# A two-layer encoder trunk: the pooled layer's group map folded into its input weights, and weights kept split between two attentions

## The chip, the cores and the metric

The kernel runs on one core of a Trainium2 chip. The core has a matrix engine (PE), three engines that work on 128 partitions (DVE, ACT and POOL), and a sequencer (SP) that issues nearly all DMAs of this kernel in one queue. The metric is the device time of one execution in microseconds; the kernel before has a median of 2261.05 us over three runs (2259.12 to 2262.42).

## The reference

Two requests (x_prompt and x_sample, 1024 tokens of 1024 channels each) go through the same two layers. Each layer computes modulation rows from c, `mod = silu(c) @ ada_w[l] + ada_b[l]`, splits them into shift, scale and gate, normalises x, applies scale and shift, mixes, normalises again and adds the gated result to x.

Layer 0 mixes by attention: one input projection of 3328 columns feeds eight heads of dilated sliding windows (the A heads) and eight heads of dense attention with two key heads (the B heads); a SiLU gate and an output projection follow. Layer 1 mixes by pooling:

```
u, gate = jnp.split(h @ w_in, 2, axis=-1)
...
pooled = win_sum / cnt - u32.reshape(b, s, POOL_GROUPS, POOL_GROUP_DIM)
mixed = jnp.einsum('bsgc,gcd->bsgd', pooled.astype(h.dtype), w_grp)
mixed = mixed * scale.reshape(POOL_GROUPS, POOL_GROUP_DIM)
y = mixed.reshape(b, s, POOL_WIDTH) * jax.nn.silu(gate)
return y @ w_out
```

There are four groups of 256 channels, with windows of 2, 4, 8 and 16 tokens. Pooling is linear along the tokens and `w_grp` is linear along the channels of a group, so the two may change places.

## The kernel before

Every large product is done on operands split in two: a value is rounded to fp32r (the high half), the rest is the low half, and three matmuls (high by high, high by low, low by high) are added up in PSUM. A weight block is 256 columns by 1024 rows; `load_block` (through `block_gen`, L354) brings it in pieces of 128 x 256 by DMA into a buffer `ws`, of which there are three, and `split` (L346) rounds each piece on DVE (L351) and subtracts on POOL (L352; on DVE for some). Two buffers `w` are used in turn.

The order of work is: the first attention (request "prompt", s = 0), its output projection (`outproj0`), the second attention (s = 1) with its output projection, then the pooled layer (`layer1`) for s = 1 and for s = 0. A scheduler of the framework may reorder instructions that don't depend on one another; `issue_after` and `keep_in_program_order` bind some of them.

**Attention (`layer0`, L641).** Thirteen projection units (one for keys and values, four "P" units for the B heads, eight "A" units), each with one weight block, are cut in 17 steps. The 64 slots of the B heads and the 32 of the A heads drive them: `adv` (L718) takes a unit one step further between the pieces of a slot, so that the block of a coming head is projected while the present head's scores, exponentials, turns and products run. P1 to P3 and A0 are stepped in the B heads' slots, a quarter of them each; A1 to A7 in the A heads'. At step 13 (`marks[-1]`) of one unit, the next one's weights are loaded. In the second attention the key-value unit and P0 run ahead of the slots; P0's weights are loaded unsplit into `raw`, early.

**Modulation rows (`ada_rest`, L214).** During P1 to P3 of the first attention, 16 blocks of 256 columns of `ada_w` are loaded and split by the same helper and multiplied (L225) with the two requests' silu(c), which stands as 34 columns of weights: four blocks for the gate of layer 0 and twelve for layer 1. A small tail per block (L152 to L158, tile `mr`) adds the bias and writes the row to DRAM. In between, `x_ahead` normalises and turns the second request's x.

**The pooled layer (`layer1`, L1202).** For each group: the projection of u (`lin`, L1213 to L1215), pooling in `pool_ct` (window sums on POOL, centring on DVE at L1264, then the split of the pooled mean, L1265 and L1266), the projection of the gate, the output product of the group before (`outp`, L1310 to L1312), and `mixed`: 24 matmuls of the pooled mean with the group's map (L1282 to L1284), the product of scale, map and gate (L1286), and its split (L1289, L1290). PSUM has four tiles "S" for all of them.

Of the kernel before, what the change touches and what calls it, by code (L numbers as in the profile page):

```python
# [13 lines left out]
P = 128  # L14
# [46 lines left out]
class Trunk:  # L61
    def __init__(self, ctx, tc, t):
# [10 lines left out]
        self.raw = None  # L73
# [18 lines left out]
        self.xn_d = self.dram.tile([KT, P, S], F32, name="xn_d")  # L92
        self.v_d = [self.dram.tile([4, 288, P], F32, name=f"v_d{i}") for i in range(3)]
# [36 lines left out]
    def ada_prep(self, pool, b):  # L130
        nc, t = self.nc, self.t
        self.apool = b
# [10 lines left out]
        nc.vector.tensor_tensor(self.cz[:, :, 32:34], csil, self.cz[:, :, 0:2].bitcast(F32), ALU.subtract)  # L143

# [69 lines left out]
    def ada_rest(self, ap):  # L214
        nc = self.nc
        todo = [(l, c, i) for l, c in ((0, 2), (1, 0), (1, 1), (1, 2)) for i in range(4)]
        cur = []

        def step(load):
# [8 lines left out]
            if load and todo:  # L228
                l, c, i = todo.pop(0)
                w = self.load_block(ap, self.ada_src(l, c, i), step=False)  # L230
                row, bias, f = (self.apool.tile([2, 256], F32, name=self.n(x), tag=x, bufs=1)
# [3 lines left out]
                cur.append((w, ps, gen))  # L235

# [117 lines left out]
    def block_gen(self, wp, sp, src, fast=False, step=True, out=None, z=1, bufs=3, tags=("ws",), act=False, raw=None):  # L354
# [6 lines left out]
        for q in range(KT // z):  # L361
            ks = slice(z * q, z * q + z)
            if raw:
                ws = raw[z * q // 4][:, z * q % 4 : z * q % 4 + z]
            else:
                ws = sp.tile([P, z, 256], F32, name=self.n("ws"), tag=tags[q % len(tags)], bufs=bufs)
                nc.sync.dma_start(ws, src[:, ks, :])
            self.split(w[:, 0, ks], w[:, 1, ks], ws, fast and q % 2 == 0, act)
            yield

    def load_block(self, wp, src, fast=False, step=True, z=1, bufs=3, raw=None):
        out = []
        for _ in self.block_gen(wp, wp, src, fast, step, out, z, bufs, raw=raw):
            pass
        return out[0]

# [76 lines left out]
    def unit_A(self, ap, subs, hT, j, out):  # L453
        nc = self.nc
        w = self.load_block(ap, self.t["win"][j])
# [32 lines left out]
        for pr in range(4):  # L488
            ps = self.ptile("J").rearrange("p (a c) -> p a c", a=2)
            yield from self.proj_tile(ps[:, 0, :], hT, w, 2 * pr)  # L490
            if pr == 2:
                trans(0)
            yield
# [49 lines left out]
    def unit_KV(self, ap, subs, hT, out):  # L543
# [21 lines left out]
        for pr in range(4):  # L565
# [4 lines left out]
            todo = []  # L570
            yield
# [23 lines left out]
    def unit_P(self, ap, subs, hT, i, out):  # L595
        nc = self.nc
        raw, self.raw = self.raw, None
        with self.tc.issue_after(self.kvd[0].ins) if raw else ExitStack():
            w = self.load_block(ap, self.t["win"][9 + i], i == 0, raw=raw, z=2 if raw else 1)
# [14 lines left out]
        for pr in range(4):  # L614
            ps = self.ptile("J").rearrange("p (a c) -> p a c", a=2)
            yield from self.proj_tile(ps[:, 0, :], hT, w, 2 * pr)
            if pr == 2:
                trans(0)
            yield
# [21 lines left out]
    def layer0(self, s, hT, ap, side, after_proj, open2, run_h, first=None):  # L641
# [15 lines left out]
        units = [(self.unit_KV(ap, subs, hT, out), 0)]  # L657
        for i in range(4):
            units.append((self.unit_P(ap, subs, hT, i, out), due[("B", 2 * i)]))
        for j in range(8):  # L660
            units.append((self.unit_A(ap, subs, hT, j, out), due[("A", j)]))
# [10 lines left out]
        if s == 1:  # L672
# [3 lines left out]
            self.raw = [ap.tile([P, 4, 256], F32, name=self.n("raw"), tag="P", bufs=3) for _ in range(2)]  # L676
            for f in range(2):
                nc.sync.dma_start(self.raw[f], self.t["win"][9][:, 4 * f : 4 * f + 4, :])
# [28 lines left out]
        with self.tc.issue_after(self.kvd[2].ins):  # L707
            next(gens[2])
# [9 lines left out]
        def adv(ui):  # L718
# [7 lines left out]
            if rest and ui in (2, 3, 4):  # L726
                if k in marks:
                    rest(k != marks[-1])
                else:
# [3 lines left out]
            if k == marks[-1] and ui + 1 < len(gens) and ui + 1 not in started:  # L733
# [338 lines left out]
    def outproj0(self, s, wo, op, hN, pre):  # L1072
# [72 lines left out]
        src = t["pwin"][0] if s else t["win"][8]  # L1145
        for i in range(NT):
            if i == 4:
                self.wi = 1
                self.kvw = self.base.tile([P, 2, KT, 256], F32R, name=self.n("w"), tag="w", bufs=1)
                for q in range(4):  # L1150
# [43 lines left out]
            if i in (5, 6):  # L1194
# [7 lines left out]
    def layer1(self, s, hT, lp, hp, run_h, open_l2):  # L1202
# [3 lines left out]
        wu0 = kvw or self.l1_block(wp, t["pwin"][0])  # L1206
# [32 lines left out]
        def pool_ct(g, ps, p):  # L1239
# [452 lines left out]
```

## Time and profile before

| what | value |
|---|---|
| median of 3 runs | 2261.05 us |
| profiled execution, its own time | 2259.73 us |
| its span | 2257.9 us |
| granted TensorE clock, mean | 0.98 of full speed |
| PE, DVE, ACT, POOL busy | 94%, 70%, 47%, 43% |
| DMA traffic | 193.26 MB, mean 86 GB/s |

The page has the busy time of each engine over the span. A table by stretch shows the same for parts of it; the attention's quarters and the pooled layer's two passes are stretches in what follows. A group of instructions is given with its line, its count, the busy time of all and the mean of one. A timeline lists instructions with their start and duration in us; a bracket behind a row gives the idle time of the engine before it and what ended that.

### The profile page before, as it was taken

The page shows a single profiled execution, that of the slowest core. Times are in us where ns is not written, and L with a number is a line of the kernel's source. Part 1 is how long each engine was busy: PE and PEld are TensorE (multiplying, and loading weights), DVE is VectorE, ACT ScalarE, POOL GpSimd, SP SyncE. Part 2 cuts the span into 40 slices and gives each one's busy share as a digit, 9 for nine tenths or more (in the row PEclk, how much of TensorE's full clock was granted, in tenths as well). Part 3 has the DMA queues.
Part 4 walks back from the last instruction along what each step waited for, and adds up shares of the span by engine and source line. Part 5 has one row for each costly group of instructions (what it writes and reads, how often), then busy time and mean ns, then how long its engine had stood idle before and what let it go on. Part 6 is the DMA issues. An engine that isn't in the chain of part 4 may idle for free.

```text
span 2257.9 us, 38531 instructions
## 1 busy us (share of the span) xinstructions
PE 2114.2 (94%) x13777; PEld 1883.1 (83%) x13777; DVE 1570.6 (70%) x3465; ACT 1065.9 (47%) x2435; POOL 973.5 (43%) x1421
## 2 busy tenths in 40 slices
PE   6998898999999799999999999998999999899998
PEld 3987788989999678998888999996787888788887
DVE  8788888767776855777777777777655455865446
ACT  6445555576666632356666666665322113211112
POOL 3676666104343512653221235334234246573452
PEclk9999999999999799999999999998999999999999
DMA  6134343102121444200011112125433234231113
GB/s 262 45 93 119 94 126 113 52 18 70 54 68 33 126 156 163 67 26 25 11 34 39 44 55 73 52 55 153 144 118 96 73 89 140 108 130 56 47 53 144
DMA packets 156640, 193.26 MB, mean 86 GB/s; under 512 B 16184, under 2 KB 117920, under 8 KB 156448
## 3 DMA queue, kind: packets, MB, share of 16 engines
q1 hardware_dynamic: 156144, 190.01, 26.5%
q8 instruction: 109, 1.79, 0.3%
q10 hardware_dynamic: 304, 0.79, 0.1%
q14 instruction: 83, 0.68, 0.1%
HBM read 148.56 MB, written 42.18 MB: 84 GB/s over the span
## 4 chain that ended last, share of the span: by engine, by line
PE 57%; DVE 20%; POOL 6%; issue 6%; ACT 5%; DMA 5%; SPq 0%; POOLq 0%; DVEq 0%; ACTq 0%
PE J L420 5%; PE J L421 5%; PE J L422 5%; PE S L1213 4%; PE S L1215 4%; PE S L1214 4%; DVE E L771 3%; POOL w L352 3%; PE H L753 3%; DVE w L351 3%; PE S L1022 3%; PE S L1023 3%; DVE mx L754 2%; PE S L1024 2%; PE T L791 2%
## 5 line engine op out<-in xcount | busy, mean ns | idle before, releaser
L352 POOL TENSOR_TENSOR w<-ws,w 128x256 fp32r<-128x256 f32 (+1 forms) x402 | 373.2, 942 | 305.1 <-DVE w L351 232.3
L420 PE MATMUL J<-w,hT 128*128 128x256 f32 x1664 | 481.0, 289 | 3.0 <-ACT xj L433 2.0
L421 PE MATMUL J<-w,hT 128*128 128x256 f32 x1664 | 477.1, 287 | 3.4 <-POOL w L352 2.6
L422 PE MATMUL J<-w,hT 128*128 128x256 f32 x1664 | 475.8, 286 | 4.3 <-DVE hT L1460 3.4
L422 PEld LDWEIGHTS J<-w,hT 128*128 128x128 f32 x1664 | 317.1, 191 | 7.6 <-DVE hT L1460 4.1
L421 PEld LDWEIGHTS J<-w,hT 128*128 128x128 f32 x1664 | 317.7, 191 | 6.5 <-POOL w L352 3.5
L420 PEld LDWEIGHTS J<-w,hT 128*128 128x128 f32 x1664 | 317.4, 191 | 6.5 <-ACT xj L433 3.3
L771 DVE TENSOR_TENSOR E<-T,E 128x512 fp32r<-128x512 f32 x384 | 261.5, 682 | 86.3 <-ACT E L770 84.1
L770 ACT ACTIVATE E<-T 128x512 fp32r<-128x512 f32 x384 | 226.7, 598 | 197.9 <-PE T L791 70.2
L351 DVE CAST w<-ws 128x256 fp32r<-128x256 f32 (+1 forms) x404 | 181.3, 473 | 142.9 <-PE S L1215 74.4
L760 ACT ACTIVATE P<-H,mx 128x512 f32<-128x512 f32 x256 | 173.8, 686 | 100.0 <-DVE mx L755 86.4
L1213 PE MATMUL S<-hT,w 128*128 128x512 f32 x512 | 201.2, 393 | 3.2 <-DVE sg L1271 2.9
L1214 PE MATMUL S<-hT,w 128*128 128x512 f32 x512 | 200.6, 392 | 0.0
L1215 PE MATMUL S<-hT,w 128*128 128x512 f32 x512 | 200.5, 392 | 0.0
L754 DVE TENSOR_REDUCE mx<-H 128x1 f32<-128x512 f32 x256 | 173.5, 681 | 33.5 <-PE H L753 31.6
L791 PE MATMUL T<-identr,P 128*128 128x128 f32 x1024 | 162.4, 274 | 8.1 <-DVE E L771 4.1
L804 PE MATMUL O<-E,v 128*128 128x256 f32 x512 | 143.1, 301 | 13.9 <-DVE E L771 13.2
L870 ACT ACTIVATE P<-H,nm 128x256 f32<-128x256 f32 x256 | 117.9, 474 | 79.5 <-DVE nm L864 79.1
L803 PE MATMUL O<-E,v 128*128 128x256 f32 x512 | 146.9, 296 | 7.6 <-ACT E L770 4.6
L791 PEld LDWEIGHTS T<-identr,P 128*128 128x128 f32 x1024 | 122.2, 141 | 24.4 <-DVE E L771 2.9
L506 POOL TENSOR_TENSOR hl<-xj,hl 128x256 fp32r<-128x256 f32 x64 | 48.4, 758 | 204.7 <-DVE hl L505 148.6
L753 PE MATMUL H<-kh,qT 128*128 128x512 f32 x256 | 112.6, 440 | 8.2 <-ACT P L760 8.1
(278 smaller groups left out, 5133.0 us busy)
## 6 DMA issues: line engine op xcount, KB each, us to landing
ws<-win SPq DMA_DIRECT2D x184, 128.0 KB
ws<-ada_w SPq DMA_DIRECT2D x128, 128.0 KB
ws<-pwin SPq DMA_DIRECT2D x60, 256.0 KB
vb<-v_d SPq DMA_DIRECT2D x64, 144.0 KB
xt<-xp SPq DMA_DIRECT2D x16, 512.0 KB
ada<-ada_w SPq DMA_DIRECT2D x16, 512.0 KB
v_d<-v SPq DMA_DIRECT2D x64, 128.0 KB
wos<-wout SPq DMA_DIRECT2D x32, 256.0 KB
```

The costliest lines, as they stand in the source:

```text
L351: nc.vector.tensor_copy(hi, src)
L352: (nc.vector if dve_lo else nc.gpsimd).tensor_tensor(lo, src, hi.bitcast(F32), ALU.subtract)
L420: nc.tensor.matmul(ps, hi, w[:, 0, k, :], start=(k == 0), stop=False)
L421: nc.tensor.matmul(ps, hi, w[:, 1, k, :], start=False, stop=False)
L422: nc.tensor.matmul(ps, lo, w[:, 0, k, :], start=False, stop=(k == KT - 1))
L754: nc.vector.tensor_reduce(mx[:, c : c + 1], ps[c], axis=AX, op=ALU.max, negate=True)
L770: nc.scalar.activation(ov[0], Tv, AF.Copy)
L771: nc.vector.tensor_tensor(ov[1], Tv, ov[0].bitcast(F32), ALU.subtract)
L791: nc.tensor.transpose(T[:, (2 * e + i) * P : (2 * e + i + 1) * P], Pt[(h, 2 * g + i)][:, (2 * kp + e) * P : (2 * kp + e + 1) * P], self.ident)
L1213: nc.tensor.matmul(ps[:, cs], w[:, 0, k, ws], hT[:, k, 0, cs], start=(k == 0), stop=False)
L1214: nc.tensor.matmul(ps[:, cs], w[:, 0, k, ws], hT[:, k, 1, cs], start=False, stop=False)
L1215: nc.tensor.matmul(ps[:, cs], w[:, 1, k, ws], hT[:, k, 0, cs], start=False, stop=(k == KT - 1))
```

## The change

The change has four parts.

First, `fold` multiplies the map of a group into the u columns of the pooled layer's input weights: for each of four groups and two halves of the rows, 24 matmuls of 256 columns, evacuated by ACT and written to DRAM as `wp_d`. The pooled layer loads `wp_d` in place of the weights; `pool_ct` leaves the pooled (and already mapped) mean in the tile `u`, unsplit, and `gated` multiplies it with scale and gate directly. The 24 matmuls of `mixed`, the split of the pooled mean and the load and split of the map go.

Second, the twelve blocks of modulation rows for layer 1 move from the first to the second attention, as 24 jobs of 128 columns. `aux` gives out these 24 jobs and the eight of the fold, three per unit from P1 to A7: at each call the job that was loaded before is multiplied, and the next is loaded and split into the one buffer `wx`.

Third, the first attention writes each of its 13 split weight blocks to DRAM (`keep_w`, in the second of a unit's four tile pairs), and the second attention reads them back in four DMAs (`w_back`) in place of loading and splitting them. The read of the next unit's block is issued at step 3 of a unit in place of step 13. The key-value block is read back during the output projection of the first attention; P0's early load into `raw` goes.

Fourth, small tiles move (tags `xt` in place of `pT`, three buffers `y1` in place of two).

```diff
-        rest = self.ada_rest(ap) if s == 0 else None
+        if s:
+            self.cz = ap.tile([P, KT, 34], F32R, name=self.n("cz"))
+            nc.sync.dma_start(self.cz.bitcast(F32), self.cz_d)
+        rest = self.ada_rest(ap, ((0, 2),)) if s == 0 else None
+        aux = self.aux(ap) if s else None
...
+            if aux and k in ((3, 8, 13) if ui < 5 else (2, 7, 12)):
+                aux()
-            if k == marks[-1] and ui + 1 < len(gens) and ui + 1 not in started:
+            if k == (3 if s else marks[-1]) and ui + 1 < len(gens) and ui + 1 not in started:
...
+    def aux(self, ap):
+        jobs = [("ada", l, c, i) for l, c in ((1, 0), (1, 1), (1, 2)) for i in range(8)]
+        jobs += [("fold", g, h) for g in range(4) for h in range(2)]
...
+            w = ap.tile([P, 2, KT, P], F32R, name=self.n("wx"), tag="wx", bufs=1)
...
+            for q in range(4):
+                ks = slice(2 * q, 2 * q + 2)
+                ws = ap.tile([P, 2, P], F32, name=self.n("ws"), tag="ws", bufs=3)
+                nc.sync.dma_start(ws, src[:, ks, :])
+                self.split(w[:, 0, ks], w[:, 1, ks], ws)
...
+                for k in range(KT):
+                    for e in range(2):
+                        nc.tensor.matmul(ps[0][0:34], self.cz[:, k, :], w[:, e, k, :], start=(k + e == 0),
+                                         stop=(k + e == KT))
...
+                        for c in range(2):
+                            q = 2 * c + kp
+                            nc.tensor.matmul(o, w[:, 0, q, at], wg[:, 0, c], start=(c == 0), stop=False)
+                            nc.tensor.matmul(o, w[:, 0, q, at], wg[:, 1, c], start=False, stop=False)
+                            nc.tensor.matmul(o, w[:, 1, q, at], wg[:, 0, c], start=False, stop=(c == 1))
...
+    def w_back(self, w, b, pin=lambda x: x):
+        for e in range(2):
+            for f in range(2):
+                sl = slice(KT // 2 * f, KT // 2 * (f + 1))
+                pin(self.nc.sync.dma_start(w[:, e, sl].bitcast(F32), self.w_d[b, :, e, sl]))
...
+    def keep_w(self, s, w, b):
+        if s == 0:
+            self.nc.sync.dma_start(self.w_d[b], w.bitcast(F32))
...
-            nc.vector.scalar_tensor_tensor(wv, wv, 1.0 / WINS[g], u[:, H : H + S], op0=ALU.mult, op1=ALU.subtract)
-            nc.scalar.activation(p[:, 0], wv, AF.Copy)
-            nc.vector.tensor_tensor(p[:, 1], wv, p[:, 0].bitcast(F32), ALU.subtract)
+            p = u[:, H : H + S]
+            nc.vector.scalar_tensor_tensor(p, wv, 1.0 / WINS[g], p, op0=ALU.mult, op1=ALU.subtract)
+            return p
...
-                for c in range(2):
-                    cs = slice(512 * c, 512 * c + 512)
-                    for k in range(2):
-                        nc.tensor.matmul(ps[:, cs], wg[:, 0, k, ws], pT[k][:, 0, cs], start=(k == 0), stop=False)
-                        nc.tensor.matmul(ps[:, cs], wg[:, 0, k, ws], pT[k][:, 1, cs], start=False, stop=False)
-                        nc.tensor.matmul(ps[:, cs], wg[:, 1, k, ws], pT[k][:, 0, cs], start=False, stop=(k == 1))
-                nc.vector.scalar_tensor_tensor(yf, ps, self.sccol[:, 2 * g + ct : 2 * g + ct + 1], sgs[ct],
+                nc.vector.scalar_tensor_tensor(yf, pm[ct], self.sccol[:, 2 * g + ct : 2 * g + ct + 1], sgs[ct],
```

## Rows read from the trace of the kernel before

**Rows 1.** The page, busy us, share of the span, instructions.
```profile
PE 2114.2 (94%) x13777; PEld 1883.1 (83%) x13777; DVE 1570.6 (70%) x3465; ACT 1065.9 (47%) x2435; POOL 973.5 (43%) x1421
```
**Rows 2.** Line 753 by stretch: PE, PEld busy (count), PEclk, DMA share, GB/s.
```profile
106.30:199.60 93.30, 21.07 (x65) 9.97 (x66) 1.00 0.35 102
```
**Rows 3.** Stretches: length, PE, PEld, DVE, ACT, POOL busy (count); PEclk, DMA, GB/s.
```profile
106.00:200.00 94.00, 84.63 (x611) 73.10 (x610) 80.94 (x189) 49.21 (x115) 67.74 (x97) 1.00 0.35 103
200.00:301.00 101.00, 88.06 (x657) 78.06 (x655) 86.40 (x196) 55.66 (x127) 64.37 (x95) 1.00 0.34 101
301.00:405.00 104.00, 96.49 (x728) 88.73 (x725) 85.06 (x199) 54.94 (x126) 64.99 (x96) 0.98 0.37 111
405.00:481.00 76.00, 70.48 (x511) 62.90 (x510) 58.65 (x139) 50.91 (x119) 10.26 (x15) 1.00 0.15 42
481.00:780.00 299.00, 279.96 (x2297) 274.36 (x2296) 219.72 (x736) 196.88 (x526) 124.00 (x259) 0.96 0.22 64
947.00:1028.00 81.00, 80.72 (x633) 76.86 (x632) 61.40 (x134) 44.76 (x105) 42.73 (x67) 1.00 0.10 31
1028.00:1105.00 77.00, 73.40 (x552) 67.41 (x551) 61.29 (x131) 49.04 (x114) 26.18 (x44) 1.00 0.08 22
1105.00:1180.00 75.00, 72.33 (x545) 66.53 (x544) 59.56 (x135) 48.34 (x113) 18.45 (x28) 1.00 0.11 30
1180.00:1250.00 70.00, 64.35 (x452) 56.03 (x451) 56.41 (x131) 49.66 (x116) 9.98 (x14) 1.00 0.11 31
1250.00:1542.00 292.00, 275.81 (x2285) 270.83 (x2284) 216.07 (x731) 195.65 (x524) 123.20 (x258) 0.96 0.22 64
1655.00:1962.00 307.00, 295.97 (x1316) 242.31 (x1315) 170.19 (x175) 65.67 (x82) 138.84 (x125) 0.98 0.31 99
1962.00:2258.00 296.00, 287.90 (x1263) 236.45 (x1261) 163.81 (x154) 46.18 (x56) 145.81 (x113) 1.00 0.26 92
```
**Rows 4.** Line 225 by stretch, columns as in rows 2.
```profile
106.30:199.60 93.30, 18.04 (x96) 10.30 (x96) 1.00 0.35 102
...
301.00:405.00 104.00, 9.75 (x64) 7.00 (x64) 0.98 0.37 111
```
**Rows 5.** Timeline of PE, four short windows: start, duration, instruction.
```profile
1785.89 0.39 PE L1282 MATMUL S<-pT,wg 128*128 128x512 f32 x1
...
1789.16 0.39 PE L1284 MATMUL S<-pT,wg 128*128 128x512 f32 x1
...
123.88 2.06 PE L225 MATMUL T<-w,cz 128*34 128x256 f32 x16
...
748.01 0.46 PE L441 MATMUL T<-identr,hl 128*128 128x128 f32 x4
748.30 0.62 PE L881 MATMUL T<-identr,P 128*128 128x128 f32 x4
```
**Rows 6.** Groups of instructions, shapes apart; the last by tile mr (min/median/max).
```profile
L1282 PE MATMUL S<-pT,wg 128*128 128x512 f32 x64 | 25.4, 396 | 0.0
...
L351 DVE CAST w<-ws 128x256 fp32r<-128x256 f32 x312 | 115.8, 391 | 45.0 <-DMA ws<-win 24.5 <-DMA ws<-ada_w 16.1 <-PE J L422 2.5
...
L352 POOL TENSOR_TENSOR w<-ws,w 128x256 fp32r<-128x256 f32 x308 | 237.0, 782 | 132.5 <-DVE w L351 112.0 <-DVE mx L755 11.2 <-DVE R L815 4.1
...
L153 DVE TENSOR_TENSOR mr<-T,mr x16: 402/404/413, 129.9 to 369.5; 2x256 f32<-2x256 f32 x16
```
**Rows 7.** Timelines of DVE and PE, end of the first pass of the pooled layer.
```profile
1939.20 1.27 DVE L1286 SCALAR_TENSOR_TENSOR yf<-S,sccol,sg 128x1024 f32<-128x1024 f32 x1
...
1941.67 0.79 PE L1310 MATMUL S<-w,y 128*128 128x512 f32 x1 [6.07 <-ACT y L1289]
```
**Rows 8.** Timeline of PE, first group of the first pass.
```profile
1713.72 0.77 PE L1213 MATMUL S<-hT,w 128*128 128x512 f32 x1 [2.94 <-DVE sg L1271]
```
**Rows 9.** Timeline of POOL, ahead of the second attention.
```profile
891.22 3.59 POOL L352 TENSOR_TENSOR w<-y,w 128x512 fp32r<-128x512 f32 x2 [9.39 <-DVE w L351]
```

More of the change, by code (lines that the diff above doesn't have):

```diff
@@ L212, in mod_rows, with ada_rest @@
         nc.sync.dma_start(self.mod_d[0, 1, 0:2].rearrange("c (k p) -> (c k) p", p=P), rows)
-    def ada_rest(self, ap):
+    def ada_rest(self, ap, todo):
         nc = self.nc
-        todo = [(l, c, i) for l, c in ((0, 2), (1, 0), (1, 1), (1, 2)) for i in range(4)]
+        todo = [(l, c, i) for l, c in todo for i in range(4)]
         cur = []
@@ L230, in step @@
                 w = self.load_block(ap, self.ada_src(l, c, i), step=False)
-                row, bias, f = (self.apool.tile([2, 256], F32, name=self.n(x), tag=x, bufs=1)
+                row, bias, f = (ap.tile([2, 256], F32, name=self.n(x), tag=x, bufs=1)
                                 for x in ("mr", "mb", "mf"))
@@ L451, in dup, with unit_A @@
         return f
-    def unit_A(self, ap, subs, hT, j, out):
+    def unit_A(self, s, ap, subs, hT, j, out):
         nc = self.nc
-        w = self.load_block(ap, self.t["win"][j])
+        w = self.win_block(s, ap, j)
         yield
@@ L541, in b_norm, with unit_KV @@
         return x
-    def unit_KV(self, ap, subs, hT, out):
+    def unit_KV(self, s, ap, subs, hT, out):
         nc = self.nc
@@ L570, in unit_KV @@
             todo = []
+            if pr == 1:
+                self.keep_w(s, w, 8)
             yield
@@ L593, in unit_KV, with unit_P @@
         yield
-    def unit_P(self, ap, subs, hT, i, out):
+    def unit_P(self, s, ap, subs, hT, i, out):
         nc = self.nc
-        raw, self.raw = self.raw, None
-        with self.tc.issue_after(self.kvd[0].ins) if raw else ExitStack():
-            w = self.load_block(ap, self.t["win"][9 + i], i == 0, raw=raw, z=2 if raw else 1)
+        w = self.win_block(s, ap, 9 + i, i == 0)
         yield
@@ L656, in layer0 @@
                 due[h] = n
-        units = [(self.unit_KV(ap, subs, hT, out), 0)]
+        units = [(self.unit_KV(s, ap, subs, hT, out), 0)]
         for i in range(4):
-            units.append((self.unit_P(ap, subs, hT, i, out), due[("B", 2 * i)]))
+            units.append((self.unit_P(s, ap, subs, hT, i, out), due[("B", 2 * i)]))
         for j in range(8):
-            units.append((self.unit_A(ap, subs, hT, j, out), due[("A", j)]))
+            units.append((self.unit_A(s, ap, subs, hT, j, out), due[("A", j)]))
         NSTEP = NT * (KT // CK) + 1
@@ L728, in adv @@
                     rest(k != marks[-1])
-                else:
+                elif ahead:
                     next(ahead, None)
@@ L1149, in outproj0 @@
                 self.kvw = self.base.tile([P, 2, KT, 256], F32R, name=self.n("w"), tag="w", bufs=1)
-                for q in range(4):
+                if s == 0:
+                    self.w_back(self.kvw, 8, pin)
+                for q in range(4 * s):
                     ws.append(tile([P, 2, 256], F32, "y0", 4))
@@ L1193, in outproj0 @@
             self.last = added
-            if i in (5, 6):
+            if s and i in (5, 6):
                 for q in (2 * i - 10, 2 * i - 9):
```

121 lines of the change are left out of this document (83 added, 38 removed).

## The prediction

> **What bounds the kernel now.** I began with the page's busy shares: PE is at 94% and DVE, the next engine, at 70% [rows 1], so the question is in which stretches PE itself is the limit. The busy table by stretch answers that. I cut it where the slots of the attention begin: 16 slots of four score matmuls each give one stretch, which the counts of L753 confirm (64 to 65 in each of eight stretches; [rows 2] has the first). The reader is to compare two attentions that do the same work [rows 3]. The second needs 81, 77, 75 and 70 us for its four quarters of B heads and 292 us for its A heads. The first needs 94, 101, 104 and 76, and 299: the A heads agree, the B heads are 72 us longer. What the first has beside them is the modulation rows (16 blocks of 256 columns: L225 has 96 matmuls in each of the first two quarters and 64 in the third [rows 4]) and the normalising of x ahead. In these three quarters DVE is busy 82 to 86% and PE 87 to 93%; in the second attention's four PE has 92 to 100%, and in its A heads it does 2285 matmuls in 292 us. The pooled layer (1655 to 2258) is PE nearly without a gap.
>
> Busy time overstates a matmul here, since the next starts before one ends. So I read prices as start-to-start distances. L1282 to L1284: from 1785.89 to 1789.16 are 14 steps, 0.234 us each [rows 5]. L225, 256 columns: 16 in 2.06 us, less one of 0.28, over 15: 0.119 us. Turning 128 columns in fp32r: 4 in 0.46 us, of 0.24 each: 0.073 us; in fp32 (4 in 0.62 us, of 0.29): 0.110 us.
>
> **The change part by part.** The sum goes against the profiled execution's 2259.7 us (span 2257.9); the median, 2261.05, is 0.06% away and is left aside.
>
> *Group map out of the pooled layer.* 192 matmuls (three lines of 64 [rows 6]), 24 per group and pass: 24 x 0.234 = 5.6 us, eight times = 44.9 us of PE. Also gone are 16 splits of the pooled mean on ACT and DVE and eight loads of the map; the gating product now reads SBUF in place of PSUM, which I price the same. PE has these matmuls alone in seven of the eight places. In the last group of the first pass it has not: PE stands 6.07 us behind the map, until 1941.67, because DVE reaches the gating product only at 1939.20, after a queue of adds, affines and casts that owes nothing to the map [rows 7]. If PE gets there earlier it stands longer: nothing gained. In the first group PE also stands, 2.94 us, for the silu product of the gate [rows 8]; I leave that stall its size. In the last group of all, the gate's chain (tanh, two products, split) loses its cover; the previous group's half of the output product is what PE can do meanwhile. Taken: 7 x 5.6 = -39. Bounds: -22 (half goes into such queues) to -48 (the first group's stall goes too).
>
> *Modulation of the pooled layer out of the first attention.* 12 of 16 blocks go: 192 matmuls x 0.119 = 22.8 us of PE, 96 casts on DVE (0.39) and 96 subtractions on POOL (0.78) [rows 6], which is 37 and 75 us, and their loads, behind which the next projection's weights stood on SP. Normalising x stays; its 64 turns cost PE 64 x 0.110 = 7 us. By quarters, the first attention is over the second by 12, 24, 29 and 6 us. The first keeps four of its six blocks: (12 - 2) x 2/6 = 3. The second and third lose all; of 24 - 2 and 29 - 2 I take 20 and 22, leaving a little for DVE's part of x. In the fourth 3 of 6. Taken: -48; bounds -23 (PE's own time) to -58 (all but the first quarter's blocks and x).
>
> *Stores of split weights.* 13 times 2.1 MB to DRAM. At 103 GB/s the DMA engines are 0.35 busy [rows 3], so some 290 GB/s are there (an estimate from that row) and a store takes 7 us, on the one SP queue, at the second of a unit's four tile pairs. Behind it on SP stand the v round trip and, later in the unit, the next unit's weights. A unit of an A head lasts some 37 us, and seven of its 17 steps, 15 us, lie between. Hidden; taken +2, bounds 0 to +15 (2 us at each of the seven A units).
>
> *Modulation into the second attention.* 24 jobs of 128 columns: 384 matmuls. No row shows a matmul of fp32r under 256 columns. Going from 512 columns (0.234) to 256 (0.119) halves the price, which carries on to 0.06; the fp32r turn of 128 columns at 0.073 lies close. Above, a 128-column matmul may cost what one of 256 does (0.119) or four times its columns, the 0.234 of a 512. I take 0.063, because the fp32r turn is the only row with these columns: 24 us; bounds 23 to 90. The Trainium skill, in "TensorE: Matmul & The Clock Gate", section "Back-to-back issue gap", gives about 81 ns for a sustained stream of 128-column matmuls with a weight load each; by that the 24 would be 31 us, and the sum 7 us later. The trace's 0.073 for a turn with a load each lies under it.
>
> *Fold into the second attention.* 8 jobs of 24 matmuls of 256 columns: 192 x 0.119 = 22.8 us, all in the A heads (steps 25 on of 33, three per unit), where PE has no room.
>
> *The rest of that attention.* 88 casts and subtractions of weights that are now read back, go; 136 for the jobs come, and 24 row tails of two or three small DVE operations of 0.40 us [rows 6]: 64 x 0.40 + 48 x 0.39 = +44 us of DVE, +37 us of POOL over 595 us, in which DVE is busy 74 to 81%, POOL under 55%. PE's queue is in order: a job's matmuls wait for POOL's last subtraction, and the score matmuls stand behind them, but a job is loaded five steps ahead (11 us of an A unit, 22 of a B unit). On SP the fourth load of a job waits for a buffer, the read-back of the next unit behind it, 14 steps early. I add 6 us in the B heads and 4 in the A heads; bounds 0 to +30 (12 jobs at the 4.5 us per block of the first attention, 72/16, over their own 24).
>
> *Start of the second attention.* KV weights come back ready: the two subtractions that ended at 894.8 [rows 9] go, worth some 3 us. Against it the first P unit's weights, formerly loaded early, can only be written once the output stage's space is free; four half-megabyte reads at 290 GB/s are 7 us, with the lows third. Taken +4, bounds -3 to +8.
>
> Sum: -39 - 48 + 2 + 24 + 23 + 10 + 4 = -24: **2236 us**. Its own range is 2218 to 2252.
>
> **The rivals.**
> *Narrow matmuls at four times the columns.* If an fp32r matmul of 128 columns streams like four passes, 384 x (0.234 - 0.063) = 66 us more, on an engine without room, in both parts of the second attention: 2301 us, slower. It decides from 0.063 + 24/384 = 0.126 us per matmul on. For it: fp32 turns cost 0.110 against 0.073, so passes do exist, and every fp32r matmul in the trace has at least 256 columns, so nothing excludes it. Against it: that turn. The Trainium skill, "FP8 and Floating Point Precision", section "TensorE Precision Notes", has true FP32 at four passes and the reduced form reading 4 bytes and truncating, and says nothing of width; by four passes it is this 2301, by one it is the forecast.
> *The second attention pays what the first paid.* The 12 blocks cost 12 x 4.5 = 54 us there instead of 34: 2256 us, within the no-change bound. For it: the same DVE and POOL work on the same queues. Against it: the first attention also loaded 11 units through the same buffers and queue, and DVE there was fuller.
> *The pooled layer gives back half.* -22 instead of -39: 2253 us. For it: the 6.07 us stall, and POOL 138 to 146 us busy in each pass. Against it: PE's union is 288 of 296 us in the second pass.
>
> **How the numbers follow.** Forecast 0.58, four passes 0.25, the other two 0.17 together. A measurement of this kernel tells 0.2% (4.5 us) from no change, that is 2255 to 2264 (around 2259.7). The forecast lies below this in 0.93 of its cases, four passes above in nearly all, the other two half below, a quarter each within and above. Faster 0.54 + 0.085 = 0.62; slower 0.25 + 0.04 + 0.02 = 0.31; same 0.07. The range must reach the four-pass case: 2216 to 2302, with some 0.07 left out below and 0.12 above.
>
> **What would show it.** Matmuls of 34 columns of weights by 128 in the second attention starting 0.06 to 0.08 us apart (forecast) or 0.2 and more (rival). The first attention's second and third quarter at 80 to 84 us; the second attention's A heads at 325 to 335 us; pooled matmuls of the next group following the gate's without a gap in seven places, and PE standing some 11 us before the last output product of the first pass. Wrong would be: those matmuls at 0.126 or more, A heads above 345 us, a first attention whose B heads stay above 345 us, or a pooled layer above 585 us.

## The result and the profile after

The changed kernel takes 2232.07 us (median of 4 runs, 2229.28 to 2233.64) beside 2260.09 (2255.91 to 2262.42) for the kernel before: ratio 0.9878 [0.9865, 0.9890]. A second measurement of the same kernel, among the experiments, gave 2238.10 and 0.9905 [0.9890, 0.9919]: from one measurement to the next a difference of 6 us tells nothing. The forecast was 2236. The profiled execution took 2229.28 us with a span of 2227.5, so its distance from the span of before, 30.4 us, is what has to be found by stage.

The page of the changed kernel, PE's share as before [rows 1], over a shorter span:

```profile
PE 2085.8 (94%) x13969; PEld 1872.4 (84%) x13969; DVE 1520.1 (68%) x3415; ACT 1060.1 (48%) x2447; POOL 915.6 (41%) x1359
```

The same stretches in the changed kernel, cut at the same slots as before [rows 3]: four quarters of the first attention's B heads, its A heads, the four quarters and the A heads of the second attention, its output stage, and the pooled layer's two passes. Columns as there:

```profile
110.00:199.00 89.00, 84.76 (x634) 76.60 (x632) 77.74 (x176) 49.31 (x113) 60.79 (x91) 1.00 0.42 128
199.00:286.00 87.00, 81.55 (x625) 75.92 (x625) 64.49 (x133) 51.49 (x117) 27.65 (x44) 1.00 0.29 98
286.00:371.00 85.00, 76.05 (x549) 67.31 (x548) 66.77 (x147) 53.56 (x124) 29.16 (x51) 1.00 0.25 81
371.00:444.00 73.00, 67.50 (x486) 59.83 (x485) 56.94 (x131) 50.16 (x116) 10.19 (x18) 1.00 0.22 70
444.00:736.00 292.00, 275.82 (x2281) 271.33 (x2280) 211.61 (x728) 195.87 (x523) 122.89 (x255) 0.97 0.31 100
...
914.00:997.00 83.00, 82.57 (x660) 78.26 (x659) 61.58 (x131) 45.94 (x108) 36.36 (x59) 1.00 0.21 68
997.00:1077.00 80.00, 76.44 (x602) 70.72 (x602) 63.70 (x138) 48.89 (x115) 28.90 (x48) 1.00 0.18 54
1077.00:1154.00 77.00, 74.72 (x591) 69.27 (x591) 62.13 (x143) 48.33 (x115) 21.27 (x33) 1.00 0.20 63
1154.00:1228.00 74.00, 67.92 (x509) 59.83 (x508) 61.51 (x147) 50.77 (x120) 12.99 (x22) 1.00 0.22 66
1228.00:1552.00 324.00, 308.78 (x2675) 303.58 (x2674) 241.46 (x809) 207.69 (x549) 157.66 (x301) 0.98 0.40 122
1569.00:1683.00 114.00, 102.53 (x470) 82.85 (x470) 59.74 (x81) 36.56 (x70) 21.82 (x40) 0.95 0.34 115
1683.00:1956.00 273.00, 272.75 (x1237) 224.77 (x1236) 157.17 (x163) 57.20 (x74) 134.58 (x121) 1.00 0.32 104
1956.00:2227.00 271.00, 262.13 (x1151) 215.56 (x1149) 146.44 (x142) 37.79 (x50) 142.67 (x109) 0.99 0.29 100
```

Taken between the same instructions (the first score matmul of the B and of the A heads, that of the A heads' last slot, the first output and the first pooled matmul), the stages stand as follows, in us. The columns of the experiments are read further down; "again" is the changed kernel measured a second time.

```
                          before  after  again  l1only  nofold  adafirst  noreload  vbws  reloadonly
start to first score       106.3  110.1  111.9   105.8   111.4     111.7     111.8 112.1       112.1
1st attention, B heads     374.8  333.5  335.4   375.5   333.2     368.8     334.3 335.4       369.8
1st attention, A heads     296.6  292.5  294.6   294.0   293.4     293.7     293.2 294.7       293.5
its end and output         111.6  112.3  110.9   110.3   111.1     113.9     111.8 111.0       113.9
start of 2nd attention      57.8   65.3   65.6    59.0    65.8      67.5      62.6  66.4        58.1
2nd attention, B heads     303.1  314.2  314.3   302.7   314.4     300.1     320.8 314.5       299.9
2nd attention, A heads     291.9  324.1  328.5   294.3   297.0     303.2     348.5 326.3       284.7
last score to output         7.9   16.7   16.6     7.7    13.7      16.5      13.2  16.8        10.8
output of 2nd attention    105.2  114.6  116.6   106.0   117.1     110.1     113.3 104.6       107.2
pooled layer, 1st pass     310.0  272.2  274.6   274.6   274.6     274.6     272.2 274.6       272.2
pooled layer, 2nd pass     285.2  263.1  261.6   261.6   261.6     261.6     263.0 261.6       263.0
end                          7.7    8.8    8.8     9.0     8.8       9.1       9.0   8.8         8.8
```

So the pooled layer gives 59.9 us and the first attention's heads 45.4; the second takes back 43.3 in its heads, 7.5 ahead of them, and 18.2 behind them (8.8 before its first output product and 9.4 in its output stage), which the prediction had not. The other 5.6 us of loss are 3.8 at the start, 0.7 in the first output and 1.1 at the end.

*The narrow matmuls.* A job's 16 matmuls in the changed kernel, in one run between other work:

```profile
952.30 1.13 PE L271 MATMUL T<-wx,cz 128*34 128x128 f32 x16
```

Less the last one's 0.22 us, 15 steps in 0.91: 0.061 us each, against the 0.063 taken; the median step of all 24 jobs is 0.060. The rival of four times the columns is dead by this row alone. The row that spoke for it, the fp32 turn at 0.110 us against 0.073, is 1.5 times and not four.

*The pooled layer's stalls.* The two places of the first pass where PE stood before [rows 7, 8], first in the kernel before, then in the changed one. The stretches are cut so that the second silu product (1712.36 and 1733.87) and the first matmul of the last output product (1941.67 and 1933.58) lie alike in them:

```profile
1700.00:1716.00 16.00, 11.28 (x48) 8.69 (x47) 7.30 (x10) 3.60 (x5) 6.22 (x7) 0.89 0.37 116
1930.00:1956.00 26.00, 19.93 (x82) 15.84 (x81) 18.98 (x17) 5.21 (x7) 10.58 (x10) 0.87 0.32 122
```

```profile
1721.00:1737.00 16.00, 16.00 (x77) 13.19 (x75) 11.97 (x11) 4.65 (x6) 5.84 (x8) 1.00 0.40 128
1922.00:1948.00 26.00, 26.00 (x116) 21.32 (x114) 23.77 (x23) 4.53 (x7) 16.21 (x7) 1.00 0.18 59
```

PE is busy throughout, and the mean granted clock of 0.89 and 0.87 is back at 1.00: behind a stall PE had run part of each stretch at the lower of its two levels (the first matmul behind each took 0.77 and 0.79 us [rows 7, 8], where one of its shape takes 0.39 [rows 5]), so a stall of 3 to 6 us cost more than its length. DVE now reaches the gating products ahead of its queue. First the map's first matmul for the last group in the kernel before, then DVE in the changed one, with one of the additions that made up the queue:

```profile
1929.84 0.39 PE L1282 MATMUL S<-pT,wg 128*128 128x512 f32 x1
```

```profile
1903.24 2.42 DVE L1378 SCALAR_TENSOR_TENSOR yf<-u,sccol,sg 128x1024 f32<-128x1024 f32 x1
...
1906.99 1.22 DVE L1382 TENSOR_TENSOR y<-yf,y 128x1024 fp32r<-128x1024 f32 x1
...
1915.18 2.34 DVE L1378 SCALAR_TENSOR_TENSOR yf<-u,sccol,sg 128x1024 f32<-128x1024 f32 x1
1917.44 1.21 DVE L1426 TENSOR_TENSOR m<-S,m 128x1024 f32<-128x1024 f32 x1
...
1937.16 1.21 DVE L1382 TENSOR_TENSOR y<-yf,y 128x1024 fp32r<-128x1024 f32 x1
```

Before, the product could not begin until the map's matmuls had run, and came at 1939.20, behind the additions, with PE waiting for it; now both products are over by 1918, and only the second one's split is late.

*The start of the second attention.* Two rows of the changed kernel show a wait there that the kernel before has not, DVE first, then PE:

```profile
879.90 0.29 DVE L428 CAST wx<-ws 128x256 fp32r<-128x256 f32 x1 [10.21 <-DMA ws<-ada_w]
```

```profile
882.80 0.49 PE L533 MATMUL T<-identr,hl 128*128 128x128 f32 x2 [8.21 <-DVE hl L675]
```

The cast of the first job's weights stands in DVE's queue 10.21 us for its load, which SP issued at 870.59, right behind the reads of a weight block and of `cz`; the split `hl` that PE turns next comes behind that cast.

### The profile page after: what moved, and what is told of

Same layout as the page of the kernel before. It is cut to its first block, busy times and chain, and to the rows that moved or that the text cites. A ratio compares the mean times of both kernels' runs of the same rounds, so it can differ in the third digit from the quotient of the medians.

```text
span 2227.5 us, 38820 instructions
## 1 busy us (share of the span) xinstructions
PE 2085.8 (94%) x13969; PEld 1872.4 (84%) x13969; DVE 1520.1 (68%) x3415; ACT 1060.1 (48%) x2447; POOL 915.6 (41%) x1359
## 5 line engine op out<-in xcount | busy, mean ns | idle before, releaser
L429 POOL TENSOR_TENSOR w<-ws,w 128x256 fp32r<-128x256 f32 (+1 forms) x218 | 228.9, 1064 | 190.7 <-DVE w L428 114.0
L428 DVE CAST w<-ws 128x256 fp32r<-128x256 f32 (+1 forms) x220 | 109.2, 526 | 117.1 <-PE S L1315 59.4
L429 POOL TENSOR_TENSOR wx<-ws,wx 128x256 fp32r<-128x256 f32 x128 | 95.6, 763 | 147.8 <-DVE wx L428 138.1
L127 POOL TENSOR_SCALAR rv<-ss 128x1 f32<-128x1 f32 x64 | 23.8, 372 | 267.1 <-ACT xe L327 94.4
```

Source lines behind the costliest of these rows:

```text
L429: (nc.vector if dve_lo else nc.gpsimd).tensor_tensor(lo, src, hi.bitcast(F32), ALU.subtract)
```

## The experiments

Theory after the result: the pooled layer gained its 45 us of matmuls plus both stalls (some 15 us), because no product there waits for the map's PSUM tiles any more; everything in the second attention is PE time and its schedule, and the saved weights matter little.

**l1only: the kernel before with the pooled layer of the changed one, the map left out.**

```diff
-        wu0 = kvw or self.l1_block(wp, t["pwin"][0])
+        wu0 = kvw
...
-            prev.append((mixed(g, pT, sgs, wg, ys), wo))
+            prev.append((gated(g, pm, sgs, ys), wo))
```

> The kernel before with the pooled layer of the changed kernel and the plain input weights: the group map is left out altogether, nothing else is changed. The sum behind the forecast had this part at -39 us (seven of eight places at 5.6 us) and the stall of 6 us at the end of the first pass staying. The two traces show -60 us over the two passes of the pooled layer, and 18 us lost ahead of it. Theory: the -60 us belong to this part alone (44.9 us of matmuls, and some 15 us of two stalls whose queues the map's PSUM tiles caused), and the 18 us to the other parts; then this kernel takes 2198 to 2206 us, and PE has no gap at either place. Rival: the passes got shorter because work ran earlier in the longer output stage ahead of them; then the passes shrink by 39 to 45 us here and it takes 2215 to 2222 us.

Measured: 2201.59 us, 0.9745 [0.9731, 0.9760]. The passes are 274.6 and 261.6 us: 59 us gone with nothing else changed, and no loss in the output stage (106.0). The theory holds but for one gap: PE still stands 2.1 us once in the last output product of the first pass, behind an addition of DVE. The pooled layer alone makes the gain; all the rest of the change together costs 30 to 36 us (ratio 0.9745 against 0.9878 and 0.9905).

**nofold: the changed kernel without the fold's jobs, the map left out.**

```diff
-        jobs += [("fold", g, h) for g in range(4) for h in range(2)]
...
-        src = self.wp_d[0]
+        src = t["pwin"][0]
```

> The changed kernel without the eight fold jobs; the pooled layer takes the plain input weights, so the map is left out. Theory: the fold costs its 192 matmuls, 22.8 us, in the A heads of the second attention, where PE has no room, and nothing elsewhere: A heads 324 to about 301 us, total 2207 to 2211 us. Rival: its loads and stores on SP also hold up the loads of the output projection (8.7 us more between the last A slot and the first output matmul than before): then the total falls by 30 to 36 us, to 2196 to 2202 us.

Measured: 2204.46, 0.9761 [0.9745, 0.9776]. The fold costs 27.6 us against the first measurement of the changed kernel (33.6 against the second). The A heads of nofold:

```profile
1229.00:1526.00 297.00, 283.93 (x2476) 279.56 (x2475) 218.05 (x768) 198.22 (x535) 127.00 (x261) 0.98 0.34 101
```

199 matmuls fewer and 27 us less than in the changed kernel, where the 192 of the fold alone account for 23 (192 x 0.119): the fold is priced by PE, with some 4 us beside. The total lies between the theory's 2207 to 2211 and the rival's 2196 to 2202: of the rival's 8.7 us ahead of the first output product, 3 came back (13.7 for 16.7).

**adafirst: the twelve modulation blocks back in the first attention, all else as changed.**

```diff
-        rest = self.ada_rest(ap, ((0, 2),)) if s == 0 else None
+        rest = self.ada_rest(ap, ((0, 2), (1, 0), (1, 1), (1, 2))) if s == 0 else None
...
-        jobs = [("ada", l, c, i) for l, c in ((1, 0), (1, 1), (1, 2)) for i in range(8)]
+        jobs = [None] * 24
```

> The changed kernel with the twelve blocks of modulation rows back in the first attention (256 columns), the fold where it is. Theory (moving them pays because DVE and SP were the limit in the first attention): the first attention's B heads return from 333 to about 375 us, the second attention loses 384 matmuls at 0.060 us = 23 us in its B and A heads and some DVE work, up to 31 us: total 10 to 20 us slower than the changed kernel, 2242 to 2252 us. Rival (the gain in the first attention came from other parts of the change): total within 5 us of the changed kernel less the 23 us, 2205 to 2214 us.

Measured: 2235.06, 0.9891 [0.9876, 0.9905], which lies between the two measurements of the changed kernel: both expectations missed. The first attention's B heads pay 35 us more (368.8), the second's B heads 14 and its A heads 21 to 25 less, its output stage 4.5 to 6.5 less. Moving the blocks was worth nothing that these runs can tell.

**noreload: the second attention splits its weights again; no stores.**

```diff
-        if s == 0:
+        if True:
             return self.load_block(wp, self.t["win"][b], fast)
...
-        if s == 0:
-            self.nc.sync.dma_start(self.w_d[b], w.bitcast(F32))
+        pass
```

> The changed kernel without the saved split weights: no block is written to DRAM in the first attention, and the second attention loads and splits all its blocks again (from step 3 of the unit before, through the same three buffers as the jobs). Theory of the forecast: DVE and POOL have room, the saving is worth 88 casts and subtractions that hide beside PE; the stores cost nothing either: within 8 us of the changed kernel, 2224 to 2240 us. Rival: with the jobs in the same buffers, POOL at twelve splits more per unit pair and SP's queue become the limit, as they were in the first attention: the second attention is longer by 25 us or more, 2257 us and up.

Measured: 2258.94, 1.0005 [0.9993, 1.0017]: the whole gain is gone. Its A heads:

```profile
1234.00:1583.00 349.00, 318.73 (x2684) 310.03 (x2682) 264.65 (x862) 208.32 (x552) 193.70 (x352) 0.97 0.35 103
```

The number of matmuls is that of the changed kernel (2684 against 2675), in 349 us in place of 324; DVE has 53 instructions more and POOL 51. So the rival was right in its price. PE stands 30 us in that stretch (349.0 less 318.7) where it stood 15 (324.0 less 308.8), most of all for `P`, which ACT makes, and ACT stands for DVE's `nm`; first noreload, then the changed kernel (us in total, times, longest):

```profile
PE H L939 <- ACT P L967: 8.2, 8, 2.0
...
ACT P L967 <- DVE nm L961: 58.3, 20, 6.3
```

```profile
PE H L940 <- ACT P L968: 1.6, 3, 1.0
...
ACT P L968 <- DVE nm L962: 45.0, 21, 5.4
```

The rival had named POOL and SP; these waits name DVE. The saved weights are worth 23 to 29 us once the jobs stand beside them (ratio 1.0005 against 0.9878 and 0.9905). Noreload also has no stores: its first attention (111.8, 334.3 and 293.2 us) is that of the changed kernel (110.1, 333.5, 292.5), so the stores cost nothing that shows.

**reloadonly: saved weights, but no jobs at all (modulation in the first attention, no fold, map left out).** It was run later, to see the same edit without the jobs.

```diff
-        jobs += [("fold", g, h) for g in range(4) for h in range(2)]
+        jobs = []
```

> The changed kernel with the modulation rows back in the first attention and no fold (plain input weights, the map left out): of the second attention's changes only the saved split weights stay. To be held against the kernel before with the changed pooled layer (2201.6 us), which differs by the saved weights alone. Theory: reading split weights back relieves the A heads by 15 to 20 us (303 us with the fold, less some 28 for it, against 294), and the places where it costs (start, first units, output stage) give back about as much: total 2198 to 2208 us. Rival (hidden anyway): A heads 290 us and more, total 2210 us and up.

Measured: 2195.77, 0.9728 [0.9712, 0.9744], 6 us under l1only, whose interval it overlaps. Its A heads, and behind them those of l1only:

```profile
1247.00:1532.00 285.00, 272.66 (x2286) 269.66 (x2284) 196.10 (x688) 196.25 (x524) 93.41 (x218) 0.98 0.28 86
```

```profile
1247.00:1542.00 295.00, 278.74 (x2287) 273.61 (x2286) 216.45 (x734) 196.19 (x525) 122.98 (x258) 0.95 0.22 63
```

Ten us less than in l1only for the same matmuls, with the first stage 6.3 us longer. The theory's 15 to 20 us in the A heads were too many, its total was missed to the good side. Without the jobs the saved weights are worth 4 to 6 us, within the noise; with them, four times that and more. The start of the second attention is 58.1 us here: reading the weights back costs nothing there by itself, and with no job no cast stands in DVE's queue. So the 7.5 us that the changed kernel lost at that place go with the first job's load. adafirst has them too (67.5): there it is a cast of the fold's map that stands 8.3 us for its load.

Part by part, then: the folded map gives 59 us and costs 28 to 34, which is about all that the change gains (28 and 21 us in the two measurements); the moved rows give nothing; the saved weights keep the jobs from costing 23 to 29 us more. The fold's jobs alone, with the rows left in the first attention and the weights split anew, were not run.

**again, vbfirst, foldfirst, both: the 18 us behind the last score.** In the changed kernel's output stage PE and SP wait as follows (us in total, times, longest):

```profile
PE T L345 <- DVE hx L333: 8.5, 2, 6.6
```

```profile
SPq L1187 <- PE O L997: 15.0, 1, 15.0
```

L1187 loads x for the output stage and L997 is the last reader of vb: with cz and wx placed ahead of it, vb must lie where the output stage's x tiles come to lie (read off this wait; the profile has no addresses), and their first load waits 15 us. Hence vbfirst, which places vb ahead of cz, and foldfirst, which takes the fold's jobs (with their stores on SP) away from the end.

```diff
         if s:
+            vb0 = [ap.tile([P, 9, P], F32R, name=self.n("vb"), tag="vb", bufs=2) for _ in range(2)]
+            for v in vb0:
+                nc.gpsimd.memset(v[:, 0, 0:1].bitcast(F32), 0.0)
             self.cz = ap.tile([P, KT, 34], F32R, name=self.n("cz"))
```

```diff
-        jobs = [("ada", l, c, i) for l, c in ((1, 0), (1, 1), (1, 2)) for i in range(8)]
-        jobs += [("fold", g, h) for g in range(4) for h in range(2)]
+        jobs = [("fold", g, h) for g in range(4) for h in range(2)]
+        jobs += [("ada", l, c, i) for l, c in ((1, 0), (1, 1), (1, 2)) for i in range(8)]
```

> The changed kernel itself, to stand beside the next three on one chip: 0.988 of the kernel before, 2232 us.

> The changed kernel, with the two buffers vb of the second attention placed ahead of the new tiles cz and wx. In the changed kernel the output stage's first load of x waits 15 us for the last product that reads vb, since the new tiles shifted vb under it; the loads behind it on SP land some 12 us later, and PE stands 9.3 us in two places for the normalised rows. Theory: that shift is the cause of the 9.5 us that the output stage lost: here x is loaded as early as before the change, the stage takes 104 us again, total 2220 to 2225 us. Rival: the loads were late because the last head ended late and DMA was busy; then no change, 2230 to 2234 us.

> The changed kernel with the order of the jobs turned round: the eight fold jobs first (in the B heads of the second attention, units P1 to P3), the modulation rows after them. Theory: in the A heads PE has no room (2285 matmuls in 292 us before), while in the B heads it stands a few per cent of the time; the A heads lose the fold's 22.8 us and get eight more jobs of 0.96 us, so they get some 15 us shorter and the tail behind them some 4 us; the B heads get some 10 to 14 us longer: total 2222 to 2228 us. Rival: PE is as full in the B heads: the same total, 2230 to 2234 us.

> Both: vb placed first, and the fold jobs first. If the two gains are apart from each other: 2210 to 2219 us.

Measured: again 2238.10, 0.9905 [0.9890, 0.9919]; vbfirst 2244.34, 0.9935 [0.9922, 0.9947]; foldfirst 2238.24, 0.9905 [0.9890, 0.9920]; both 2235.15, 0.9896 [0.9883, 0.9910]. vbfirst and both missed what was expected; foldfirst came out as its rival had it, at the time of the changed kernel beside it.

vbfirst made it worse, and SP shows why: now ws lies under the x tiles, and the load (L1190 there) waits longer, for another reader (L1166 reads a tile in ws's buffers).

```profile
SPq L1190 <- DVE yw L1166: 24.3, 1, 24.3
```

The output stage went to 123.7 us. So this form of the theory fell. Its mechanism can be read in all 14 traces, from when the first and the third load of x are issued, counted from the first output product (us). Six runs have both within 12 us, and stages of 104.6 to 108.4. In two only the third is late (110.1 and 114.5). In six the first is 16 us late or more, and the later it is, the longer the stage, up to 123.7.

```
             first x load  third x load  output stage
nolast               -0.1           7.7         104.8
vbws                  1.7           7.8         104.6
before                6.6           8.4         105.2
l1only                6.6           8.4         106.0
reloadonly            4.8           6.6         107.2
vbwsff                4.7          11.1         108.4
adafirst              1.7          25.7         110.1
both                  4.7          29.8         114.5
noreload             16.3          18.3         113.3
after                16.7          18.6         114.6
again                16.7          18.6         116.6
nofold               19.3          21.3         117.1
foldfirst            20.6          22.6         118.5
vbfirst              26.0          27.8         123.7
```

foldfirst makes the B heads 17 us longer (331.5) and the A heads 9 to 13 shorter (315.0), takes 6 off the stretch before the output (10.7) and adds 2 to 4 to the output stage; in sum nothing.

**vbws, vbwsff: vb and ws both ahead of cz; the second with the fold first too.**

```diff
+            early = [ap.tile([P, 9, P], F32R, name=self.n("vb"), tag="vb", bufs=2) for _ in range(2)]
+            early += [ap.tile([P, 256], F32R, name=self.n("ws"), tag="ws", bufs=3) for _ in range(3)]
```

> The changed kernel with the buffers vb and ws of the second attention both placed ahead of cz and wx. With vb alone placed first, the first load of x in the output stage waited 24.3 us for the last reader of ws instead of 15 us for that of vb, and the stage took 123.7 us instead of 114.6 and 116.6. With both first, x should come to lie over wx, whose last reader ends some 50 us before. Theory (the wait of that load makes the stage longer): the load waits for neither, its wait is under 5 us, the stage takes 104 to 107 us, total 2222 to 2229 us. Rival (the stage is longer for another reason and the longer wait of the last run was a side effect): the wait goes and the stage still takes 112 us or more, total 2232 to 2240 us.

> The same with the fold jobs first. The order of the jobs by itself was worth nothing (B heads +17 us, A heads -13 us, the tail -6 us), so with the load's wait gone the total should be that of the kernel beside it, 2220 to 2229 us.

Measured: vbws 2226.49 (2225.57 to 2228.80), 0.9862 [0.9843, 0.9882]; vbwsff 2229.39, 0.9876 [0.9860, 0.9892], a little above its range. The output stage of vbws and what PE waited for in it:

```profile
1577.00:1681.00 104.00, 100.53 (x470) 81.50 (x469) 59.66 (x81) 36.50 (x72) 22.20 (x41) 0.99 0.37 126
```

```profile
PE T L345 <- DVE hx L333: 0.5, 1, 0.5
```

The same 470 matmuls in 104 us in place of 114, clock 0.99 in place of 0.95, and 0.5 us of that wait in place of 8.5. The loads of x (L1191 there) wait 3.5 us at most now; the wait behind `yw` (17.0 us) falls on a load of y, and PE doesn't feel it. So the 9.4 us of the output stage were where a tile lies. By its time vbws is ahead of both measurements of the changed kernel; its interval is clear of the second (0.9890 to 0.9919) and overlaps the first, and the changed kernel was not measured beside it, so the stage shows the gain better than the total.

**nolast: vbws, and no job in the last A unit.**

```diff
-            if aux and k in ((3, 8, 13) if ui < 5 else (2, 7, 12)):
+            if aux and ui < 12 and k in ((3, 8, 13) if ui < 5 else (2, 6, 10, 14) if ui < 8 else (2, 7, 12)):
```

> The kernel that has the vb and ws buffers placed ahead of cz and wx, with one more edit: the first three A units take four jobs each (steps 2, 6, 10, 14) in place of three, so that the last A unit has none. It asks where the 8.7 us between the last score slot and the first output product come from (16.7 us in the changed kernel, 16.8 with the buffers moved, 7.9 before). Theory: the fold's evacuated result and the output weights' raw tiles share a tag of two buffers, and both stand on the one SP queue behind the fold's own loads; the output weights' first load is issued 22.5 us before the last slot (1529.6 against 1552.1) in place of 28.5 us (1513.4 against 1541.9) in the kernel before, and their 16 casts and subtractions fall among the last reductions on DVE. Without jobs in the last unit the first load is back at 27 us or more ahead, and the stretch at 8 to 12 us; A heads 320 to 330, in all 2217 to 2223 us. Rival: the stretch is long because the slots themselves come later against the projections, whatever loads; then it stays at 14 us or more and the time at 2224 to 2230.

Measured: 2228.07, 0.9874 [0.9856, 0.9893]. The output weights' loads, first the changed kernel's, then nolast's (number, duration in ns as least, median and most, first and last start):

```profile
L1105 SPq DMA_DIRECT2D wos<-wout x16: 327/328/418, 1529.6 to 1556.0; - x16
```

```profile
L1109 SPq DMA_DIRECT2D wos<-wout x16: 327/330/526, 1532.7 to 1564.5; - x16
```

The last score slot of nolast is at 1561.8, so the first load is 29 us ahead of it, as the theory wanted, and the stretch is still 15.7 us: the theory fell. The time is in the rival's range, and the traces speak for it. The stretch from the last score slot to the first output product, in the kernel before, the changed one, nolast and foldfirst:

```profile
1541.90:1549.80 7.90, 4.87 (x33) 3.87 (x31) 7.90 (x19) 4.17 (x13) 5.13 (x4) 0.92 0.57 151
```

```profile
1552.10:1568.70 16.60, 8.31 (x47) 7.27 (x46) 14.12 (x37) 9.72 (x30) 8.90 (x14) 0.71 0.57 164
```

```profile
1561.80:1577.40 15.60, 8.61 (x47) 7.61 (x47) 14.29 (x37) 9.10 (x26) 7.37 (x12) 0.72 0.54 154
```

```profile
1564.10:1574.70 10.60, 5.16 (x34) 4.05 (x32) 10.59 (x29) 5.44 (x17) 5.21 (x5) 0.98 0.48 144
```

PE has 14 matmuls more to do there in the changed kernel and in nolast, turns and products of the last head that were done ahead of its last scores before. With the fold away from the end most of them go again. What sets them back, with no job in the last unit, is open. The output stage stayed at 104.8.

## Why the prediction held, and where it didn't

The time was right to 4 us, partly because errors cancelled: that it was so near is luck.

- *Map out of the pooled layer:* -59.9 us against -39, outside the bound of -48, which had eight places and the first stall in it (44.9 + 2.9), though its words name the stall alone. The matmuls' own price held: the second pass has four groups' worth, 4 x 5.6 = 22.5, and gave 22.1. The step that failed is that of the stall at [rows 7] ("If PE gets there earlier it stands longer: nothing gained") and of the one at [rows 8]. Both went, 15 us of the first pass's 37.8, and l1only shows it with nothing else changed; the forecast's sign, PE standing some 11 us before the last output product, did not come. For the stall at [rows 7] I had looked at the queue ahead of the gating product and not at what put the product there: its operand came out of PE. With the operand already in SBUF, DVE does it before the queue. Why the one at [rows 8] went is not shown: the map no longer takes a PSUM tile there, and the splits of the pooled mean are gone from ACT and DVE as well.
- *Modulation out of the first attention:* -41.3 in the B heads against -48; the second and third quarter came to 88 and 85 us where 80 to 84 was said. adafirst gives 35 of it to the twelve blocks.
- *Modulation into the second attention:* the price of a matmul held (0.061). With adafirst beside it the move costs 35 to 40 us in the heads, near the forecast's 34 and under the rival's 54, and some 5 in the output stage. But by adafirst it brought 35 and not 48, so moving the blocks, which the sum had at a gain of 14, was worth nothing.
- *Fold:* +23 by matmuls; nofold gives 28 to 34 with all that hangs on it.
- *The rest of that attention:* heads together +43.3 against 57 (24 + 23 + 10). I had counted the weights' casts and subtractions as work that hides anyway; noreload says that they don't where the jobs stand.
- *Stores of split weights:* +2 said, nothing measured: noreload has none and is no shorter there. The start is 3.8 us longer in the changed kernel, and 4 to 6 in every run with its attention, with the stores or without; which edit does that, no run separates.
- *Start of the second attention:* +7.5 against +4, and not for the reason given: reloadonly reads the weights back at no cost, and the changed kernel's trace has DVE standing 10.2 us for the first job's load, with PE 8.2 us behind it.
- *Not forecast at all:* +18.2 behind the last score. 9.4 of it is the x load that came to wait for a reader of the tile that must have lain there before; 8.8 are 14 matmuls of the last head that came to stand behind its last scores, and the waits among them, with the cause open.

So -21 in the pooled layer and -14 in the second attention's heads stood against +18 behind it, +7 that the first attention gave less, and smaller ones, and the sum was 6 us off its place by the profiled spans (-30.4 against -24).

## What to carry to other kernels

A matmul that is folded away ahead of time can give back not only its own time but a wait for its result: look in the trace for what the consumer would do with the operand already there. An edit that inserts tiles into a pool can move those behind it, and the first loads of the next stage can come to wait for a new last reader; the queue's own waits show that, no engine's busy share does. A cast that is set early into an engine's queue holds up what stands behind it until its load has come. Work that hides beside one load of an engine can stop hiding beside two: saved weights were worth 4 to 6 us alone and 23 to 29 with the jobs.

## What the runs showed of the hardware

The gating product took 1.27 to 1.29 us in all of 16 cases with an operand in PSUM; the mean is 2.0 us with all in SBUF. I had priced the two the same. Two of them in the changed kernel, DVE first, then POOL:

```profile
1724.71 1.29 DVE L1378 SCALAR_TENSOR_TENSOR yf<-u,sccol,sg 128x1024 f32<-128x1024 f32 x1
...
1735.11 2.32 DVE L1378 SCALAR_TENSOR_TENSOR yf<-u,sccol,sg 128x1024 f32<-128x1024 f32 x1
```

```profile
1726.12 0.10 POOL L1342 MEMSET u<- 128x8 f32 x1 [4.26 <-DVE yf L1378]
...
1732.27 4.09 POOL L429 TENSOR_TENSOR w<-ws,w 128x512 fp32r<-128x512 f32 x3 [2.34 <-DVE w L428]
1737.50 0.32 POOL L1342 MEMSET u<- 128x8 f32 x1 [1.14 <-DVE yf L1378]
```

At 1724.71 POOL stands and the product takes 1.29 us. At 1735.11 POOL is in its third subtraction until 1736.36, and the product ends 1.07 us after that: it waited. Of the 16 products with all in SBUF, the ten that took 2.2 to 3.4 us began with POOL in an operation; the others took 1.28 to 1.29, one of them with POOL at work for its first 0.2 us. In the kernel before, eight of the 16 also began with POOL in an operation, and took no longer. The Trainium skill, "SBUF — State Buffer", section "SBUF: two separate sides", says that a DVE operation with two SBUF inputs and a GpSimd one that reads SBUF exclude each other for a whole instruction; these rows agree. It cost PE nothing that shows: the second pass gave 22.1 of the matmuls' 22.5 us.
